# Layer 2: VectorE turns the probabilities in 32x32 blocks, DMAs exchange the groups of 32 partitions by way of DRAM, and GpSimd makes the low parts

## The chip, the cores and the metric

The kernel runs on one core of a Trainium2 chip. The metric is the device time of one execution in microseconds (us), as a median of several runs. The engines are called by their names in the profile: PE (TensorE, matmuls and transposes), DVE (VectorE), ACT (ScalarE), POOL (GpSimd) and SP (SyncE, which issues all the DMAs here). Each engine works through its own list in a fixed order; an instruction that has to wait holds up all that stand behind it on its engine.

## What is computed

A two-layer encoder over 1024 tokens of width 1024, in fp32. Both layers run projections, several attentions, a gate and an output projection. The change touches the attentions of layer 2:

```python
def odd_layer(x, mem_n, ...):
    h = rmsnorm(x, norm_g)
    q1, q2, k1, k2, v, xq, gate = _split(h @ w_in, ODD_SPLITS)
    lam = ...
    y_c = diff_attention_blocked(q1, q2, k1, k2, v, lam, table)   # 6 heads
    y_c = rmsnorm(y_c, subln_g) * (1.0 - lam_init)
    y_x = memory_cross_attention(xq, mem_n, w_mem_kv)             # 4 heads
    y = jnp.concatenate([y_c, y_x], axis=-1) * jax.nn.silu(gate)
    return x + y @ w_out

def diff_attention_blocked(q1, q2, k1, k2, v, lam, table):
    # for each head and each block of 128 queries
    s = einsum("ibqhd,ibshd->ibhqs", qi, kk) * D ** -0.5
    p = softmax(s + bias)
    w = p[0] - lam * p[1]
    return einsum("bhqs,bshe->bqhe", w, v)
```

## The kernel before

Every fp32 operand of a large product is split into a high part (rounded to PE's fp32r) and a low part (the rest), and a product is the sum of two or three products of such parts. The sequence is 8 blocks of 128 queries.

**Steps and pairs.** Layer 2 runs 8 steps of memory attention (four heads side by side, 256 memory tokens each) and then 6 heads × 8 steps of differential attention, one step per query block. Two steps of neighbouring blocks form a pair: 4 pairs, then 24. In all these steps a tile e of 128 queries x 1024 fp32 probabilities has to be transposed, so that the product with the values can sum over the keys: PE does this in 8 transposes of 128x128 (te, L580), each half of them into one PSUM tile; ACT rounds the half to the high part (L347), DVE subtracts it to give the low part (L348). The parts go into the tiles PT. There is one PT per pair.

**The loop.** `run_steps` (L475) writes the program. Its iteration i writes, for several steps at once: the hooks (loads of weights; `early.step`, which splits a piece of the output weights, wor on load, wos on ACT L270 and POOL L271); the hop of step i−1, a DMA that copies the finished e into a tile er of the type that PE's transposes want (`word_copy`); the scores of step i (sc, L1505 and L1514), bias and minimum on DVE (L1520), Exp on ACT (L1523); matmuls of the projections of later heads as filling (acc, L329, whose weights wr are split by DVE into wh, L241, and by POOL into wl, L243); the posts of an earlier pair; s3, the product of a pair with the values (oc, 16 matmuls, L1545 and L1547), lag + 1 iterations after the step; s2, the transposes, lag iterations after it; and the finish of step i on DVE (L1528 to L1532), which makes e = p0 − c·p1. The lag is 2.

**Behind oc.** ACT copies half of the sum out of PSUM (L1550), DVE adds the other half to give O (L1551). The post d1 sums squares on PE (ssqc, L1563) and POOL takes the power −1/2 (rz2, L231). The post d2 spreads that over the partitions on PE (rbcc, L1576), DVE multiplies O with it (L1578), and POOL multiplies into the gate tile (gy, L1581).

**Order and buffers.** The functions above give the order in which the program is written; a scheduler of the language then decides the order on each engine, within the dependences. `issue_after` sets one instruction behind another. The finish of a step is set so behind the last subtraction of s2 (`late=True`, `behind`). oc and acc share two PSUM buffers (tag A), the scores have two, PT one per half, er two, wr and wor share two.

Of the kernel before, what the change touches and what calls it, by code (L numbers as in the profile page):

```python
# [12 lines left out]
F32 = mybir.dt.float32  # L13
F32R = mybir.dt.float32r
AF = mybir.ActivationFunctionType
ALU = mybir.AluOpType
AX = mybir.AxisListType

P = 128
S = 1024  # L20
# [135 lines left out]
def encoder_kernel(ctx, tc, A):  # L156
# [39 lines left out]
    for t in (spare, edge):  # L196
# [12 lines left out]
    memT_d = [dr.tile([P, KT, MEM], F32R, name="memT%d" % i) for i in range(2)]  # L209
    wo_d = [[[dr.tile([P, 8, 512], F32R, name="wo%d%d%s" % (l, nh, c)) for c in "hl"] for nh in range(2)]  # L210
            for l in range(2)]
    vec_d = dr.tile([6, 512], F32, name="vec_d")
    skew_d = dr.tile([6, P, 512], F32, name="skew_d")

# [174 lines left out]

    def open_main(stack, side, l):  # L390
        M = Main()
        M.ne, M.xbufs = 0, 0
        M.wide = l == 1
        M.pl = pool(stack, "main%d" % l, side)
        M.cfg = (dict(Q=(1024, 4), K=4, KL=4, V=1, gy=4, sg=3, er=3) if l == 0
                 else dict(Q=(512, 8), K=4, KL=2, V=2, gy=2, sg=5, er=2))
        return M
# [77 lines left out]
    def run_steps(steps, jobs, hooks=None, pace=None):  # L475
        n = len(steps)
        posts = deque()
        p2 = p3 = 0
        finish = None
        for i in range(n + LAG + 1):  # L480
            behind = None
            if jobs is not None:
                jobs.step = i
            if hooks:
                hooks(i)
            if 0 < i <= n and steps[i - 1].hop:
                steps[i - 1].hop()
            if i < n:
                if steps[i].need:
                    jobs.ensure(*steps[i].need)  # L490
                finish = steps[i].s1()
            f = steps[min(i, n - 1)].fill
            if jobs is not None:
                if half[0] and len(wout) >= 8 and jobs.projected():
                    f = pace(i)
                two = f > 1 and p3 < n and p3 + steps[p3].lag + 1 <= i and steps[p3].s3b is not None
                jobs.pull(f - f // 2 - two)
                if hooks:
                    hooks(-1)
            for q in list(posts):  # L500
                q.pop(0)()
                if not q:
                    posts.remove(q)
            if p3 < n and p3 + steps[p3].lag + 1 <= i:
                st, p3 = steps[p3], p3 + 1
                if st.s3 is not None:
                    if st.need3:
                        jobs.ensure(*st.need3)
                    r = st.s3()
                    if r:  # L510
                        posts.append(r)
                    if st.s3b is not None:
                        jobs.pull(two)
                        st.s3b()
            if p2 < n and p2 + steps[p2].lag <= i:
                behind = steps[p2].s2()
                p2 += 1
            if finish:
                with (tc.issue_after(behind.ins) if behind is not None else nullcontext()):
                    finish()  # L520
                finish = None
            if jobs is not None:
                jobs.pull(f // 2)
                if hooks:
                    hooks(-1)
        while posts:
            for q in list(posts):
                q.pop(0)()
                if not q:
                    posts.remove(q)  # L530

    class Step:
# [2 lines left out]
        need3 = ()  # L535
        lag = 2
        hop = None
        s3 = None
        fill = 0

# [26 lines left out]
            e[0] = t  # L567
        return f

    def dense_s2(M, e, st, late=False):  # L570
        def f():
            if st.sub == 0:
                st.grp["pt"] = new_pt(M)
            h, lo = st.grp["pt"]
            for j in range(2):
                T = ps_t("te")
                to, idt = (T.bitcast(F32R), identr) if e[0].dtype == F32R else (T, ident)
                for i in range(4):
                    k = 4 * j + i
                    nc.tensor.transpose(to[:, i * P:(i + 1) * P], e[0][:, k * P:(k + 1) * P], idt)  # L580
                Tv = T.rearrange("p (k c) -> p k c", k=4)
                o = slice(st.sub * P, st.sub * P + P)
                r = split_to(h[:, 4 * j:4 * j + 4, o], lo[:, 4 * j:4 * j + 4, o], Tv)
            return r if late else None
        return f

    def mem_jobs(M, l, memT, X):
# [21 lines left out]
    def x_steps(M, X, gates, fill, qtile, ydst):  # L609
        steps = []  # L610
        for qb in range(8):
            st = Step()
            st.sub = qb % 2
            if st.sub == 0:
                grp = {}
            st.grp = grp
            e = [None]
            st.fill = fill

            def s1(qb=qb, e=e):  # L620
                kh, kl = X["kh"], X["kl"]
                Sp = ps_s("sx").rearrange("p (h m) -> p h m", h=4)
                for h in range(4):
                    qt, qc = qtile(h, qb)
                    qk(Sp[:, XPOS[h], :], qt, qc, kh[:, h, :], kl[:, h, :], 0, MEM)
                mn = stat("mn4", 4)
                nc.vector.tensor_reduce(out=mn, in_=Sp, op=ALU.min, axis=AX.X)
                et = new_e(M)
                ev = et.rearrange("p (h m) -> p h m", h=4)
                z = stat("z4", 4)  # L630
                for h in range(4):
                    nc.scalar.activation(ev[:, h, :], Sp[:, h, :], AF.Exp, bias=mn[:, h:h + 1],
                                         scale=-1.0, accum_out=z[:, h:h + 1])
                def finish():
                    rz = stat("rz4", 4)
                    nc.vector.reciprocal(rz, z)
                    for h in range(4):
                        nc.scalar.activation(ev[:, h, :], ev[:, h, :], AF.Copy, scale=rz[:, h:h + 1])
                    e[0] = et
                return finish  # L640
            st.s1 = s1
            st.hop = word_copy(M, e)
            st.s2 = dense_s2(M, e, st)
            if st.sub == 1:
                def s3(qb=qb, grp=grp):
                    v = X["v"]
                    ph, pl_ = grp["pt"]
                    S2 = ps_s("ox")
                    for p in range(2):
                        acc = S2[:, p * 512:p * 512 + 512]  # L650
                        for j in range(2):
                            h = 2 * p + j
                            n = 0
                            for kt in range(2):
                                for pt in (ph, pl_):
                                    nc.tensor.matmul(acc[:, j * 256:j * 256 + 256], v[:, kt, h, :],  # L656
                                                     pt[:, 2 * XPOS[h] + kt, :], start=(n == 0), stop=(n == 3))
                                    n += 1
                    for p in range(2):
                        acc = S2[:, p * 512:p * 512 + 512]  # L660
                        t = M.at.tile([P, 256], F32, tag="yt", name="yt", bufs=2)
                        for j in range(2):
                            a = slice(j * 64, j * 64 + 64)
                            nc.scalar.copy(t[a, :], acc[64 - j * 64:128 - j * 64, j * 256:j * 256 + 256])
                        for j in range(2):
                            a = slice(j * 64, j * 64 + 64)
                            nc.vector.tensor_tensor(out=t[a, :], in0=acc[a, j * 256:j * 256 + 256], in1=t[a, :],
                                                    op=ALU.add)
                        g = gates[6 + p][:, (qb - 1) * P:(qb + 1) * P]
# [812 lines left out]
    for h in range(6):  # L1482
        for qb in range(8):
# [8 lines left out]
            def s1(h=h, qb=qb, e=e, grp=grp):  # L1492
# [33 lines left out]
                def finish():  # L1526
# [4 lines left out]
                                                   op0=ALU.mult, op1=ALU.mult)  # L1531
                    nc.vector.scalar_tensor_tensor(out=es[0], in0=es[1], scalar=c, in1=es[0],  # L1532
                                                   op0=ALU.mult, op1=ALU.add)
                    e[0] = es[0]
                return finish
            st.s1 = s1
            st.hop = word_copy(M, e)
            st.s2 = dense_s2(M, e, st, True)
            if st.sub == 1:
                def s3(h=h, qb=qb, grp=grp):  # L1540
                    ph, pl_ = grp["pt"]
# [132 lines left out]
```

## Time and profile before

| | |
|---|---|
| three runs | 1223.57, 1226.14, 1230.64 us; median 1226.14 |
| the profiled execution's span | 1228.9 us |
| PE busy in it | 1196.5 us (97%) |
| DVE, ACT, POOL busy | 801.1 (65%), 663.1 (54%), 436.3 (36%) |
| layer 2's attention | about 680 to 1162 us of the span |
| the output projection of layer 2 behind it | from 1161.95 us on |

The profile is of one execution. A line "L329 PE MATMUL acc<-h,wh ..." names the line of the kernel that is printed above, the engine, the operation and the tiles; behind the bar stand the busy time and the mean duration in ns, and then how long the engine was idle just before such instructions and who released it. The chain of waits follows the end of the execution back, at each step to what released the instruction.

### The profile page before, as it was taken

How to read it: one execution, taken by the hardware profiler on the slowest of the kernel's cores; microseconds unless marked ns; L12 is line 12 of the kernel's file. 1: busy time of each engine (PE TensorE's matmuls, PEld its weight loads, DVE VectorE, ACT ScalarE, POOL GpSimd, SP SyncE). 2: the span in 40 equal slices, each digit the busy share in tenths (PEclk: the TensorE clock that was granted, in tenths of full speed). 3: DMA queues.
4: the chain of work that ended last, by engine and by line, in shares of the span. 5: the costliest groups of instructions: out<-in, count | busy, mean ns of one | idle time of the engine just before them, and what ended most of it. 6: DMA issues, size and time to landing. Idle time of an engine off the chain costs nothing.

```text
span 1228.9 us, 19560 instructions
## 1 busy us (share of the span) xinstructions
PE 1196.5 (97%) x6614; PEld 988.4 (80%) x6614; DVE 801.1 (65%) x1495; ACT 663.1 (54%) x1477; POOL 436.3 (36%) x414
## 2 busy tenths in 40 slices
PE   6999999999999999999999999999999999999997
PEld 5788888888888777888888777777787777777886
DVE  5547665377778878635365866766767767667544
ACT  6248754366667766636157744555545454445332
POOL 5023365366665455437112222333143231301100
PEclk9999999999999999999999999999999999999999
DMA  6664445545465565457645445355363452468354
GB/s 257 200 194 147 163 172 163 166 160 207 163 233 209 208 227 191 151 196 237 186 158 156 153 146 164 121 183 163 124 187 125 153 171 105 149 212 285 121 192 155
DMA packets 114304, 216.70 MB, mean 176 GB/s; under 512 B 13302, under 2 KB 47478, under 8 KB 114204
## 3 DMA queue, kind: packets, MB, share of 16 engines
q1 hardware_dynamic: 114060, 215.25, 52.5%
q8 instruction: 53, 0.87, 0.3%
q14 instruction: 47, 0.39, 0.1%
q10 hardware_dynamic: 144, 0.20, 0.0%
HBM read 87.71 MB, written 39.86 MB: 104 GB/s over the span
## 4 chain that ended last, share of the span: by engine, by line
PE 47%; DVE 2%; DMA 1%; issue 1%; ACT 1%; POOL 0%; POOLq 0%; SPq 0%; DVEq 0%; ACTq 0%
PE acc L329 24%; PE po L702 5%; PE oc L1545 3%; PE sc L1505 3%; PE te L580 3%; PE sc L1514 2%; PE pre L702 2%; PE oc L1547 2%; DMA wr<-in_w_in 1%; PE ssqc L1563 1%; PE ox L656 0%; PE rbcc L1576 0%; PE tv L439 0%; PE sx L543 0%; DVE e L1520 0%
## 5 line engine op out<-in xcount | busy, mean ns | idle before, releaser
L329 PE MATMUL acc<-h,wh 128*128 128x512 f32 x1536 | 499.5, 398 | 1.6 <-DVE h L351 0.8
L329 PEld LDWEIGHTS acc<-h,wh 128*128 128x128 f32 x1536 | 282.4, 188 | 65.7 <-issue 7.9
L329 PE MATMUL acc<-h,wl 128*128 128x512 f32 x768 | 303.8, 396 | 1.5 <-POOL wl L243 1.2
L243 POOL TENSOR_TENSOR wl<-wr,wh 128x512 fp32r<-128x512 f32 x94 | 124.8, 1329 | 286.3 <-DVE wh L241 155.0
L1523 ACT ACTIVATE e<-e,mn 128x1024 f32<-128x1024 f32 x96 | 110.0, 1148 | 117.0 <-DVE mn L1520 116.9
L329 PEld LDWEIGHTS acc<-h,wl 128*128 128x128 f32 x768 | 144.3, 188 | 34.9 <-issue 4.4
L1114 POOL TENSOR_TENSOR e<-e,rz 128x1024 f32<-128x1024 f32 x48 | 91.6, 1910 | 84.2 <-DVE rz L1113 57.8
L1520 DVE CUSTOM_DVE_ANT_0 e<-sc,toep 128x1024 f32<-128x1024 f32 x96 | 113.5, 1218 | 8.0 <-PE sc L1514 7.3
L580 PEld LDWEIGHTS te<-identr,er 128*128 128x128 f32 x896 | 92.2, 143 | 18.8 <-PE sa L543 2.2
L580 PE MATMUL te<-identr,er 128*128 128x128 f32 x896 | 99.9, 246 | 4.3 <-DVE O L1578 1.4
L348 DVE TENSOR_TENSOR PT<-te,PT 128x512 fp32r<-128x512 f32 x112 | 74.3, 687 | 42.8 <-ACT PT L347 39.2
L241 DVE CAST wh<-wr 128x512 fp32r<-128x512 f32 x112 | 58.2, 522 | 42.9 <-PE acc L329 17.3
L348 DVE TENSOR_TENSOR PTl<-te,PTh 128x512 fp32r<-128x512 f32 x112 | 74.0, 684 | 9.4 <-ACT PTh L347 8.9
L1545 PE MATMUL oc<-PT,v 128*128 128x512 f32 x192 | 69.8, 403 | 0.7 <-DVE ckl L1420 0.7
L1532 DVE SCALAR_TENSOR_TENSOR e<-e,mr 128x1024 f32<-128x1024 f32 x48 | 66.3, 1381 | 1.5
L347 ACT CAST PT<-te 128x512 fp32r<-128x512 f32 x112 | 62.7, 589 | 7.2 <-PE te L580 6.7
L347 ACT CAST PTh<-te 128x512 fp32r<-128x512 f32 x112 | 62.2, 586 | 7.9 <-PE te L580 7.1
L702 PE MATMUL po<-woh,yh 128*128 128x512 f32 (+1 forms) x172 | 65.7, 382 | 0.0
L702 PE MATMUL po<-woh,yl 128*128 128x512 f32 (+1 forms) x172 | 65.5, 381 | 0.0
L702 PE MATMUL po<-wol,yh 128*128 128x512 f32 (+1 forms) x172 | 65.3, 380 | 0.0
L1105 DVE TENSOR_REDUCE mn<-sb 128x1 f32<-128x1024 f32 x48 | 58.3, 1216 | 7.0 <-PE sb L543 6.6
L350 ACT ACTIVATE yh<-yr 128x256 fp32r<-128x256 f32 (+2 forms) x56 | 24.0, 447 | 66.2 <-DMA yr<-ysc 37.5
(211 smaller groups left out, 2358.7 us busy)
## 6 DMA issues: line engine op xcount, KB each, us to landing
er<-e SPq DMA_DIRECT2D x112, 512.0 KB, 3.0
wr<-in_w_in SPq DMA_DIRECT2D x96, 256.0 KB, 3.0
ysc<-gy SPq DMA_DIRECT2D x16, 512.0 KB, 2.7
cq<-sg SPq DMA_DIRECT2D x64, 128.0 KB, 2.5
ck<-sg SPq DMA_DIRECT2D x48, 128.0 KB, 2.3
er<-e SPq DMA_DIRECT2D x12, 384.5 KB, 2.6
xpsc<-xh SPq DMA_DIRECT2D x18, 256.0 KB, 2.6
xr<-xpsc SPq DMA_DIRECT2D x9, 512.0 KB, 3.6
```

Source lines behind the costliest of these rows:

```text
L243: (nc.vector if fast else nc.gpsimd).tensor_tensor(out=lo, in0=raw, in1=hi, op=ALU.subtract)
L329: lastmm[0] = nc.tensor.matmul(acc, a, b[:, k, c0:c0 + n], start=(i == 0), stop=(i == 23))
L347: nc.scalar.copy(hi, src)
L348: return nc.vector.tensor_tensor(out=lo, in0=src, in1=hi, op=ALU.subtract)
L580: nc.tensor.transpose(to[:, i * P:(i + 1) * P], e[0][:, k * P:(k + 1) * P], idt)
L702: lastmm[0] = nc.tensor.matmul(acc, a, b, start=(start and n == 0), stop=(stop and n == 2))
L1105: nc.vector.tensor_reduce(out=mn, in_=Sp, op=ALU.min, axis=AX.X)
L1114: nc.gpsimd.tensor_tensor(out=et, in0=et, in1=rz.to_broadcast([P, 1024]), op=ALU.mult)
L1520: nc.vector.tensor_tensor_reduce(out=et, in0=Sp, in1=toeps[h][:, w0:w0 + 1024], scale=1.0, scalar=BIG, op0=ALU.add, op1=ALU.min, accum_out ...
L1523: nc.scalar.activation(et, et, AF.Exp, bias=mn[:, m:m + 1], scale=-1.0, accum_out=z[:, m:m + 1])
L1532: nc.vector.scalar_tensor_tensor(out=es[0], in0=es[1], scalar=c, in1=es[0], op0=ALU.mult, op1=ALU.add)
L1545: nc.tensor.matmul(acc, V[:, kt, 0, :], ph.both[:, kt, :], start=(kt == 0), stop=(kt == 7), skip_group_check=True)
```

## The change

In layer 2 alone (`M.wide`), PE's transposes are replaced by three steps that together give the same tiles PT:

1. At the end of the finish DVE turns e within blocks of 32x32 in one instruction, into the second e tile of the step (`blocks_turned`, L575 of the changed kernel). The blocks are laid out so that the 1024 words of a partition are four runs of 256.
2. The hop writes that tile to DRAM (`turned_out`, 512 KB per step; three buffers that take a pair each). A new entry, fetch, two iterations after the step, reads it back for both steps of a pair, once per pair: four DMAs of 256 KB, each for 32 partitions in runs of 256 words, which exchanges the groups of 32 partitions (`turned_in`). There is one er tile for a pair.
3. s2 has no PE work: ACT rounds from er to the high part (L607), four times a pair, and POOL subtracts to give the low part (L608), four times a pair, instead of DVE (`turned_s2`).

The lag is 3 instead of 2, so s2 comes three iterations after the step and oc four. The `late` ordering is gone. Below line 570 the changed kernel's lines are higher by 52 as a rule (L1581 is L1633), above it by one.

```diff
@@ run_steps
             if 0 < i <= n and steps[i - 1].hop:
                 steps[i - 1].hop()
+            if 1 < i <= n + 1 and steps[i - 2].fetch:
+                steps[i - 2].fetch()
...
+    turn_d = [dr.tile([2, P, S], F32, name="turn_d%d" % i) for i in range(3)]
...
+    def blocks_turned(dst, src):
+        nc.vector.transpose(out=dst.rearrange("p (c k j) -> p k c j", c=4, k=8),
+                            in_=src.rearrange("p (k c j) -> p k c j", c=4, k=8))
+
+    def turned_out(M, e, st):
+        def f():
+            if st.sub == 0:
+                M.nturn = (M.nturn + 1) % len(turn_d)
+            st.grp["turn"] = turn_d[M.nturn]
+            dma(st.grp["turn"][st.sub], e[0])
+        return f
+
+    def turned_in(M, st):
+        def f():
+            if st.sub == 0:
+                return
+            t = M.at.tile([P, 2, 4, 256], F32, tag="er", name="er", bufs=1)
+            src = st.grp["turn"].rearrange("s (g i) (c x) -> c i (s g) x", g=4, c=4)
+            for c in range(4):
+                dma(t[32 * c:32 * c + 32].rearrange("p s g x -> p (s g) x"), src[c])
+            st.grp["er"] = t
+        return f
+
+    def turned_s2(st):
+        def f():
+            if st.sub == 0:
+                st.grp["pt"] = new_pt(M)
+            h, lo = st.grp["pt"]
+            er = st.grp["er"][:, st.sub].rearrange("p g (k j) -> p k g j", k=8)
+            for j in range(2):
+                ks = slice(4 * j, 4 * j + 4)
+                o = slice(st.sub * P, st.sub * P + P)
+                hv, lv = (t[:, ks, o].rearrange("p k (g j) -> p k g j", g=4) for t in (h, lo))
+                nc.scalar.copy(hv, er[:, ks])
+                nc.gpsimd.tensor_tensor(out=lv, in0=er[:, ks], in1=hv, op=ALU.subtract)
+        return f
+
+    def turn_pairs(M, e, st):
+        st.lag = 3
+        st.hop = turned_out(M, e, st)
+        st.fetch = turned_in(M, st)
+        st.s2 = turned_s2(st)
...
@@ the steps of memory attention, at the end of finish
                     e[0] = et
+                    if M.wide:
+                        e[0] = new_e(M)
+                        blocks_turned(e[0], et)
...
-            st.hop = word_copy(M, e)
-            st.s2 = dense_s2(M, e, st)
+            if M.wide:
+                turn_pairs(M, e, st)
+            else:
+                st.hop = word_copy(M, e)
+                st.s2 = dense_s2(M, e, st)
...
@@ the steps of differential attention
-                    e[0] = es[0]
+                    blocks_turned(es[1], es[0])
+                    e[0] = es[1]
...
-            st.hop = word_copy(M, e)
-            st.s2 = dense_s2(M, e, st, True)
+            turn_pairs(M, e, st)
```

The order on three engines at one place, the first pair of the fourth head, where the head before ends. On POOL before, from the power of one pair (rz2) to that of the next (gy is the product into the gate, wos and wl are low parts of weights, toep the bias of the next head):

```order
L231 TENSOR_TENSOR rz2_10905<-z2_10902,nhalf_78 128x2
L271 TENSOR_TENSOR wos_10945<-wor_10943,wos_10945 128x256
L243 TENSOR_TENSOR wl_10971<-wr_10968,wh_10970 128x512
L1581 TENSOR_TENSOR gy_10573<-O_10813,gy_10573 128x256
L243 TENSOR_TENSOR wl_10977<-wr_10974,wh_10976 128x512
L271 TENSOR_TENSOR wos_11069<-wor_11067,wos_11069 128x256
L1474 COPY toep_11295<-far_83 128x768 x2
L231 TENSOR_TENSOR rz2_11114<-z2_11111,nhalf_78 128x2
```

Here POOL has only gate products and weights, and behind gy stand pieces of weights. On POOL after:

```order
L232 TENSOR_TENSOR rz2_10732<-z2_10729,nhalf_78 128x2
L1526 COPY toep_10981<-far_83 128x768 x2
L1633 TENSOR_TENSOR gy_10332<-O_10637,gy_10332 128x256
L608 TENSOR_TENSOR PT_10644<-er_10575,PT_10644 128x4x128
L608 TENSOR_TENSOR PT_10645<-er_10575,PT_10645 128x4x128
L608 TENSOR_TENSOR PT_10644<-er_10575,PT_10644 128x4x128
L608 TENSOR_TENSOR PT_10645<-er_10575,PT_10645 128x4x128
L272 TENSOR_TENSOR wos_10675<-wor_10673,wos_10675 128x256
L244 TENSOR_TENSOR wl_10700<-wr_10697,wh_10699 128x512
L244 TENSOR_TENSOR wl_10706<-wr_10703,wh_10705 128x512
```

The four low parts of the next pair (two tiles PT, two steps) now stand on POOL, and they stand behind the gy product of the pair before them.

On PE before, at the same place, with the last filling, rbcc of the one pair and the start of oc of the next:

```order
L329 MATMUL acc<-h,wl 128x512
L329 MATMUL acc<-h,wh 128x512
L1576 MATMUL rbcc<-ident,rz_10905 128x128 x2
L1545 MATMUL oc<-PT,v 128x512
L1547 MATMUL oc<-PT,v 128x256
L1545 MATMUL oc<-PT,v 128x512
```

Here oc stands directly behind rbcc. On PE after:

```order
L330 MATMUL acc<-h,wh 128x512
L1628 MATMUL rbcc<-ident,rz_10732 128x128 x2
L330 MATMUL acc<-h,wh 128x512
L330 MATMUL acc<-h,wl 128x512
L330 MATMUL acc<-h,wh 128x512 x2
L330 MATMUL acc<-h,wl 128x512
L330 MATMUL acc<-h,wh 128x512 x2
L330 MATMUL acc<-h,wl 128x512
L1597 MATMUL oc<-PT,v 128x512
L1599 MATMUL oc<-PT,v 128x256
```

Eight matmuls of the projections (acc) now stand between rbcc and oc.

On DVE before, around the two instructions that deal with O:

```order
L241 CAST wh_10970<-wr_10968 128x512
L1578 SCALAR_TENSOR_TENSOR O_10813<-O_10813,misc_84,rbcc_10997 128x256
L241 CAST wh_10976<-wr_10974 128x512
L1551 TENSOR_TENSOR O_11019<-oc_11002,O_11019 128x256
L348 TENSOR_TENSOR PT_11026<-te_11028,PT_11026 128x4x128
L348 TENSOR_TENSOR PT_11027<-te_11035,PT_11027 128x4x128
L1528 RECIPROCAL rz_11042<-mn_10950 128x1
L1530 SCALAR_TENSOR_TENSOR mr_11044<-mn_10950,misc_84,rz_11042 128x1
```

Here one cast stands between O's multiplication and the addition of the next O, and the low parts of PT follow. On DVE after:

```order
L1584 SCALAR_TENSOR_TENSOR e_10786<-e_10789,mr_10846,e_10786 128x1024
L575 STREAM_TRANSPOSE e_10789<-e_10786 128x8x4x32
L1630 SCALAR_TENSOR_TENSOR O_10637<-O_10637,misc_84,rbcc_10809 128x256
L352 SCALAR_TENSOR_TENSOR sg_10753<-acc_10709,sg_10752 128x512
L242 CAST wh_10699<-wr_10697 128x512
L242 CAST wh_10705<-wr_10703 128x512
L1603 TENSOR_TENSOR O_10831<-oc_10814,O_10831 128x256
L352 SCALAR_TENSOR_TENSOR sg_10859<-acc_10792,sg_10858 128x512
```

The low parts of PT are gone from DVE; the turn (STREAM_TRANSPOSE) stands ahead of O's multiplication, and two casts of weights and one of the projection's results stand between that and the addition of the next O.

More of the change, by code (lines that the diff above doesn't have):

```diff
@@ L391, in open_main @@
         M = Main()
-        M.ne, M.xbufs = 0, 0
+        M.ne, M.xbufs, M.nturn = 0, 0, 0
         M.wide = l == 1
@@ L537, in encoder_kernel @@
         hop = None
+        fetch = None
         s3 = None
@@ L568, in word_copy, with dense_s2 @@
         return f
-    def dense_s2(M, e, st, late=False):
+    def blocks_turned(dst, src):
[36 more added lines that the diff above has]
+        st.s2 = turned_s2(st)
+    def dense_s2(M, e, st):
         def f():
@@ L582, in f @@
                 o = slice(st.sub * P, st.sub * P + P)
-                r = split_to(h[:, 4 * j:4 * j + 4, o], lo[:, 4 * j:4 * j + 4, o], Tv)
-            return r if late else None
+                split_to(h[:, 4 * j:4 * j + 4, o], lo[:, 4 * j:4 * j + 4, o], Tv)
         return f
```

## Prediction

> **What bounds the kernel now.** I read the busy table of the stages first, then the chain of waits inside one stage, then the groups by line there, then what POOL waits for.
>
> ```profile
> core 0: us, PE busy (x) PEld busy (x) DVE busy (x) ACT busy (x) POOL busy (x), PEclk, DMA share, GB/s
> 680.00:1162.00 482.00, 478.79 (x2537) 378.27 (x2537) 338.31 (x615) 243.30 (x496) 125.49 (x131) 1.00 0.49 161
> ```
>
> The stretch from 680 to 1162 us is the attention of layer 2, where nearly all of the change lies. PE is busy for 478.79 of 482 us at full clock, so it sets the pace: what PE no longer does is gained whole, and each microsecond that PE waits is lost whole. DVE has 30% of the stretch free, POOL 74%.
>
> ```profile
> 906.22 0.38 PE te L580 x4
> 906.60 0.53 PE acc L329 x2
> 907.13 0.29 PE te L580 x4
> ...
> 910.70 0.91 PE sc L1505 x4
> 911.60 0.66 PE sc L1514 x4
> 912.26 3.86 PE acc L329 x16
> 916.12 0.22 PE rbcc L1576 x2
> 916.34 0.23 PE oc L1545
> 916.57 0.12 PE oc L1547
> ...
> 919.13 0.65 PE te L580 x8
> 919.78 1.92 PE acc L329 x8
> ```
>
> This is the chain of waits for the steps around 910 us (start, length, what). It never leaves PE. One pair of query blocks holds 16 transposes te, 0.38 + 0.29 + 0.65 = **1.32 us**, and the products oc, 16 matmuls of (0.23 + 0.12) a couple, 2.80 us in all, stand straight behind rbcc. An oc reads PT, whose low part DVE made long before, so nothing holds it.
>
> **What goes.** Layer 2 has 4 pairs of memory attention and 24 of differential attention: 28 × 1.32 = **37.0 us** of PE go. Since the chain runs through every te, I count all of it.
>
> **DVE and ACT.** Per step two PT subtractions (L348) leave DVE and one turn of 128x1024 comes.
>
> ```profile
> L348 DVE TENSOR_TENSOR PT<-te,PT 128x512 fp32r<-128x512 f32 x100 | 66.5, 688 | 40.3 <-ACT PT L347 36.8
> L347 ACT CAST PT<-te 128x512 fp32r<-128x512 f32 x100 | 56.3, 589 | 6.6 <-PE te L580 6.2
> L1532 DVE SCALAR_TENSOR_TENSOR e<-e,mr 128x1024 f32<-128x1024 f32 x48 | 66.3, 1381 | 1.5
> L241 DVE CAST wh<-wr 128x512 fp32r<-128x512 f32 x40 | 17.8, 446 | 12.9 <-DMA wr<-in_w_in 9.8 <-PE acc L329 1.9 <-issue 0.9
> ```
>
> The third column group is busy time and mean ns. No turn stands in the trace. It lies between two casts of 512 (2 × 0.446 = 0.89) and the L1532 pass over 1024 (1.38). I take 1.22, as nearer to the full pass because both move 1024 words a lane in one instruction. DVE then gives 1.38 and takes 1.22: even, and DVE has room at both ends. The Trainium skill ("VectorE: DVE Perf Modes", § The three transpose paths) speaks against a change of this kind: VectorE's transpose makes separate 32x32 blocks only, TensorE's a whole 128x128, and a plain DMA that does a transpose by strides is 19 times slower than the DMA's own transpose when the inner destination stride is large. Here the DMAs exchange runs of 256 words, not single words, so its condition is not met; by that rule a fetch would never be hidden, and no row here shows such a DMA. ACT's casts stay (589 ns from PSUM, from SBUF hardly more); ACT is 50% busy.
>
> **POOL.** Four subtractions of 128x512 a pair move to POOL. The same operation at the same size stands there as wl.
>
> ```profile
> L243 POOL TENSOR_TENSOR wl<-wr,wh x94: 1259/1290/2377, 12.8 to 1068.5; 128x512 fp32r<-128x512 f32 x94
> L271 POOL TENSOR_TENSOR wos<-wor,wos 128x256 fp32r<-128x256 f32 x32 | 27.4, 858 | 49.5 <-ACT wos L270 49.1
> L1114 POOL TENSOR_TENSOR e<-e,rz 128x1024 f32<-128x1024 f32 x48 | 91.6, 1910 | 84.2 <-DVE rz L1113 57.8
> L1474 POOL COPY toep<-far 128x768 f32<-128x768 f32 x8 | 6.4, 827 | 14.6 <-DVE mn L1520 14.6
> POOL gy L1581 <- DVE O L1578: 78.5, 19, 7.5
> ```
>
> The first row has min/median/max ns. I take the median, **1.29 us**, each; the new one differs in strides alone. The lower end is half of L1114 (0.96), the upper 2.38. Per pair that is 5.2 us more on POOL, which has some 15 of 20 free. Its busy time is no bound; its order is. The last row says that gy waited for DVE's O 19 times in this execution, up to 7.5 us. Before, nothing urgent stood behind gy. In the changed order the four subtractions of pair p+1 stand behind the gy of pair p in 13 of 24 pairs, and in those PE comes to oc of pair p+1 after little else than rbcc of pair p. How long gy takes from rbcc is in the timeline:
>
> ```profile
> 1014.95 0.38 PE L1576 MATMUL rbcc<-ident,rz 128*128 128x128 f32 x2
> 1015.60 0.48 DVE L1578 SCALAR_TENSOR_TENSOR O<-O,misc,rbcc 128x256 f32<-128x256 f32 x1
> 1016.16 0.75 POOL L1581 TENSOR_TENSOR gy<-O,gy 128x256 f32<-128x256 f32 x1 [5.46 <-DVE O L1578]
> ```
>
> From the start of rbcc to the end of gy: 1016.91 − 1014.95 = 1.96 us. The first oc needs the first half of both blocks, three subtractions: 3 × 1.29 = 3.87. So oc may start **5.83 us** after rbcc. PE has rbcc itself (0.22) and what stands between. The list, pair by pair of the order:
> - three pairs with 8 acc between (1.92): 5.83 − 0.22 − 1.92 = 3.69 each, 11.1;
> - the first pair with a toep copy (0.83) and two wl (2.58) among the subtractions: 4.5 before the first oc, and (2.58 + 1.29 − 1.40) = 2.5 before the second half of them, 7.0;
> - one with a subtraction already ahead of gy: 2.4; one with 8 acc and two score matmuls between (2.4): 3.2; two with 8 acc and ten score matmuls (3.9) but one wos (0.86) ahead of the fourth subtraction: 2.4 each, 4.8;
> - the last three pairs of the program, with four, four and two po matmuls (0.23 each) between: 4.7, 4.7, 5.1, together 14.5;
> - two with 8 us or more between: nothing.
>
> Sum **43 us**, against nothing before (the chain above shows rbcc and oc adjoining). If PE itself is late, its rbcc is late as well and the distance stays.
>
> **The accumulators.** oc and the projections' acc share two PSUM buffers, and an oc buffer is free when DVE has added O (L1551). Before, 14 of 24 O adds stand straight behind O's multiplication on DVE, most others with one cast between. Now 13 of 24 have the 128x1024 pass (L1532) within two rows ahead, and others two casts whose loads wait on SP for POOL's reads. At the low end the pass is done before oc's 2.80 us are over: nothing. At the upper end one pass of 1.28 to 1.38 in each of the 24 pairs: 31 to 33 us. I take half, **16 us**, since oc's 2.80 us hide the multiplication and about one of the two long instructions.
>
> **The DMAs.**
>
> ```profile
> er<-e SPq DMA_DIRECT2D x48, 512.0 KB, 2.9
> woh<-wo10h SPq DMA_DIRECT2D x8, 256.0 KB, 4.9
> wol<-wo10l SPq DMA_DIRECT2D x8, 256.0 KB, 5.6
> wr<-in_w_in SPq DMA_DIRECT2D x40, 256.0 KB, 3.2
> ...
> L175 SPq DMA_DIRECT2D er<-e x136: 464/472/614, 77.2 to 1146.0; - x136
> ...
> SPq L175 <- DVE e L1532: 78.6, 32, 9.8
> ```
>
> The hop stays one issue per step, to DRAM instead of SBUF (2.9 us; the 16 engines are half busy). New are four issues of 256 KB a pair, behind the hop on SP. The reads from DRAM land in 3.2 to 5.6 us, and SP takes 0.47 an issue. I take 3.2 + 4 × 0.47 = 5.1, with 7.5 as the other end. The last row shows how SP already stands still for DVE's e, 32 times; the loads wr and wor behind it then wait too. The third step of lag covers 10 us (482 us over 48 steps), so I put nothing on the pairs, and **5 us** on the two ends, where the first and the last pair meet the longer way (turn 1.22, fetch 5.1, three subtractions 3.87, less the 3.4 below that are idle already and some 2 of po): between 0 and 10.
>
> ```profile
> 1157.38 3.39 issue
> 1160.77 0.70 POOL rz L231
> ```
>
> **Sum.** −37.0 + 43 + 16 + 5 = +27 on the profiled span of 1228.9 is 1256. That execution lay 2.8 above the median of the runs (1226.14) and inside their spread; taken off, **1253 us**, 2.2% slower.
>
> **Rivals.**
> *GpSimd is quick enough: faster.* Place: the stretch from gy to the first oc in the 13 pairs. Price: each 0.1 us of a subtraction is worth some 3.5 us, as some 35 subtractions in all stand between a gy and an oc that waits. With 16 for the accumulators gone and 5 for the ends, it decides from about 0.98 us per subtraction; at 0.75, what gy takes for half the size, the sum is −37 + 24 + 5 = −8, 1218 us. For it: L1114 does 512 words in 0.96. Against it: 94 wl of the same operation never took less than 1.259.
> *The waits at oc and no more: a draw.* The adds are in time and the ends cost nothing to 5: −37 + 43 + 3 = +9 at most, or less if a few of the 13 waits are shorter: 1226 to 1235, taken at 1231. For it: DVE has 30% free.
> *The round trip or POOL is slow: much slower.* There is one er tile for a pair, so the next fetch waits for the last subtraction. With fetches of 10 us instead of 5.1 some 3 us per pair come on top wherever POOL has no time in hand: 12 to 24 pairs, 36 to 72, 1289 and more. The same comes of subtractions of 1.7 us when they collide with DVE's passes: 35 × 0.4 = 14 directly, and as much again through the accumulators. Two rows show such a collision:
>
> ```profile
> 1048.96 1.28 DVE L1532 SCALAR_TENSOR_TENSOR e<-e,mr 128x1024 f32<-128x1024 f32 x1
> 1049.03 2.38 POOL L243 TENSOR_TENSOR wl<-wr,wh 128x512 fp32r<-128x512 f32 x1 [1.95 <-DMA wr<-in_w_in]
> ```
>
> POOL's wl began 0.07 us behind DVE's pass and took 2.38 instead of 1.29, as if it had stood still until the pass was over. The Trainium skill ("SBUF — State Buffer", § SBUF: two separate sides) says just that: a VectorE instruction with two SBUF inputs and a GpSimd one that reads SBUF exclude each other for a whole instruction. These two rows agree with it; by that rule each of the 48 passes that meets a subtraction costs one of the two up to 1.3 us.
> *The change does not do what it says*: not so, the rows of the order have no te in layer 2.
>
> **How the numbers follow.** Forecast 0.62, gain 0.15, draw 0.08, much slower 0.15. The forecast's own range comes from the accumulators' 0 to 33 and the ends' 0 to 10: 1232 to 1275. The range reaches to 1215 and 1288 and leaves out about half of the gain and most of the much slower case. A change within 0.5% (6 us) can't be told from none with this kernel's runs; the draw lies across that bound. Faster 0.15, same 0.10, slower 0.75.
>
> **What would show it.** Right: te gone from layer 2 with 37 us of PE; PE idle ahead of oc with POOL's subtraction as releaser, some 40 us over about 13 pairs, and nothing like it in the others; the new POOL row at 1.29; PE idle ahead of acc with DVE's O add as releaser, about 16. Wrong: POOL rows below 1 us; PE waiting for oc in none of the 13; or fetches that land in 10 us and POOL's subtractions waiting for er.

## The result, and the profile after

| | before | after |
|---|---|---|
| median of the runs | 1227.06 us (4 runs, 1223.57 to 1230.64) | 1391.53 us (4 runs, 1385.1 to 1393.86) |
| ratio | | 1.134, 95% interval 1.130 to 1.137 |
| profiled span | 1228.9 us | 1392.1 us |
| granted TensorE clock, mean over the span | 0.996 | 0.931 |

The change makes the kernel 164 us slower, six times what was forecast (27) and outside the range (1215 to 1288). First the busy table by stretches, of the changed kernel (busy us of each engine with the count of instructions, then granted clock, DMA share, GB/s):

```profile
core 0: us, PE busy (x) PEld busy (x) DVE busy (x) ACT busy (x) POOL busy (x), PEclk, DMA share, GB/s
0.00:640.00 640.00, 617.22 (x3564) 524.16 (x3565) 416.00 (x789) 374.13 (x857) 297.74 (x266) 1.00 0.56 191
640.00:850.00 210.00, 153.42 (x661) 118.29 (x660) 110.04 (x166) 86.06 (x196) 82.19 (x72) 0.82 0.50 143
850.00:1150.00 300.00, 258.86 (x1139) 195.87 (x1138) 188.68 (x302) 129.51 (x262) 151.18 (x132) 0.93 0.58 171
1150.00:1392.00 242.00, 190.87 (x807) 147.39 (x806) 110.45 (x183) 75.12 (x163) 62.53 (x57) 0.85 0.55 174
```

Layer 1, up to 640 us, is as it was. From there on no engine is full: PE at 73, 86 and 79% (before: 99% in the attention), DVE at 46 to 63%. What bounds the kernel is no longer an engine, but engines that wait for each other. And the clock, which was 1.00 in this stage, stands at 0.82 to 0.93 in these stretches.

The whole can be accounted for on PE. For each matmul from 640 us on I took the time to the start of the next one: the median of its kind in the kernel before is work, a small excess is slow clock, a larger one is waiting (where the border between the two is set moves some 3 us from one to the other). Work went from 587 to 547 us (−40: te is gone), waiting from 4 to 169 (+165), slow clock from 2 to 41 (+39). Together +164.

Then the groups by line (busy, mean ns, idle before), and what engines waited for (us in total, times, longest), of the changed kernel:

```profile
L608 POOL TENSOR_TENSOR PT<-er,PT 128x512 fp32r<-128x512 f32 x112 | 151.8, 1382 | 95.4 <-ACT PT L607 94.7 <-DMA xh<-x1sc 0.7
L575 DVE STREAM_TRANSPOSE e<-e 128x1024 f32<-128x1024 f32 x53 | 65.8, 1241 | 9.7 <-ACT e L684 8.8
L1597 PE MATMUL oc<-PT,v 128*128 128x512 f32 x192 | 86.4, 477 | 37.8 <-POOL PT L608 37.1 <-DVE gy L461 0.7
```

```profile
...
POOL PT L608 <- ACT PT L607: 94.7, 16, 16.9
...
DVE wh L242 <- DMA wr<-in_w_in: 62.9, 17, 14.5
...
ACT wos L271 <- DMA wor<-in_w_out: 38.5, 17, 7.5
PE oc L1597 <- POOL PT L608: 37.1, 11, 6.0
...
PE sc L1557 <- DVE mn L1572: 27.2, 14, 5.0
```

The durations are as forecast: a turn 1.24 us, a subtraction 1.38. PE's wait at oc for POOL's subtractions is there too, 37.1 us in 11 waits, and 43 was forecast. That looks like a hit and isn't one, as the experiments show. The new rows are the others. DVE's casts of weights wait 62.9 us for the load (9.8 in the attention before), ACT's for wor, POOL for ACT. One such place, in the timeline (start, length; the idle time before it and its releaser in brackets):

```profile
799.48 0.26 ACT L1619 ACTIVATE z<-ssqc,es 128x1 f32<-128x1 f32 x1 [8.13 <-PE ssqc L1615]
799.63 1.13 ACT L607 CAST PT<-er 128x512 fp32r<-128x512 f32 x2
800.32 2.49 POOL L608 TENSOR_TENSOR PT<-er,PT 128x512 fp32r<-128x512 f32 x2 [16.89 <-ACT PT L607]
...
805.87 2.48 POOL L244 TENSOR_TENSOR wl<-wr,wh 128x512 fp32r<-128x512 f32 x2
...
808.38 0.33 SPq L175 DMA_DIRECT2D wr<-in_w_in  x1
...
811.28 0.43 DVE L242 CAST wh<-wr 128x512 fp32r<-128x512 f32 x1 [14.46 <-DMA wr<-in_w_in]
811.62 1.28 DVE L352 SCALAR_TENSOR_TENSOR sg<-acc,sg 128x512 fp32r<-128x512 f32 x2
...
812.36 1.22 PE L330 MATMUL acc<-h,wh 128*128 128x512 f32 x2 [12.92 <-DVE sg L352]
```

Read from the end: PE stands still for 12.92 us because DVE hasn't emptied an accumulator (sg). DVE could have, but a cast of weights stands ahead of it in DVE's list and waits 14.46 us for its load. The load goes out at 808.38, when POOL's wl has freed its buffer. POOL is late because a subtraction ahead of wl waited 16.89 us for ACT's cast of PT, and that stood in ACT's list behind z, which waited 8.13 us for PE's ssqc. No instruction here is long. Each list holds something back behind a thing that isn't needed yet.

### The profile page after: what moved, and what is told of

Read it like the earlier page. It is cut to its first block, busy times and chain, and to the rows that moved or that the text cites. A ratio compares the mean times of both kernels' runs of the same rounds, so it can differ in the third digit from the quotient of the medians.

```text
span 1392.1 us, 18783 instructions
## 1 busy us (share of the span) xinstructions
PE 1220.4 (88%) x6166; PEld 985.7 (71%) x6166; DVE 825.2 (59%) x1439; ACT 664.8 (48%) x1477; POOL 593.6 (43%) x526
## 4 chain that ended last, share of the span: by engine, by line
PE 24%; issue 10%; POOL 8%; DMA 8%; DVE 5%; SPq 2%; ACT 2%; POOLq 0%; DVEq 0%; ACTq 0%
PE acc L330 12%; POOL PT L608 6%; PE po L754 4%; DMA er<-turn_d 3%; SPq L175 2%; PE oc L1597 2%; DMA wor<-in_w_out 1%; DMA wr<-in_w_in 1%; DVE e L1584 1%; PE sc L1566 1%; PE pre L754 1%; PE sc L1557 1%; PE oc L1599 1%; POOL wl L244 1%; DVE e L1572 1%
## 5 line engine op out<-in xcount | busy, mean ns | idle before, releaser
L330 PE MATMUL acc<-h,wh 128*128 128x512 f32 x1536 | 510.1, 407 | 35.9 <-DVE sg L352 12.9
L330 PEld LDWEIGHTS acc<-h,wh 128*128 128x128 f32 x1536 | 293.0, 194 | 106.6 <-DVE sg L352 13.0
L608 POOL TENSOR_TENSOR PT<-er,PT 128x512 fp32r<-128x512 f32 x112 | 151.8, 1382 | 95.4 <-ACT PT L607 94.7
L242 DVE CAST wh<-wr 128x512 fp32r<-128x512 f32 x112 | 69.1, 623 | 92.0 <-DMA wr<-in_w_in 70.5
L1597 PE MATMUL oc<-PT,v 128*128 128x512 f32 x192 | 86.4, 477 | 37.8 <-POOL PT L608 37.1
L1557 PE MATMUL sc<-ck,cq 128*128 128x512 f32 x192 | 64.8, 440 | 37.1 <-DVE mn L1572 27.2
L232 POOL TENSOR_TENSOR rz<-z,nhalf 128x2 f32<-128x2 f32 x24 | 22.2, 926 | 147.0 <-ACT z L1619 147.0
L1597 PEld LDWEIGHTS oc<-PT,v 128*128 128x128 f32 x192 | 44.3, 231 | 53.7 <-POOL PT L608 41.7
L575 DVE STREAM_TRANSPOSE e<-e 128x1024 f32<-128x1024 f32 x56 | 69.5, 1240 | 9.7 <-ACT e L684 8.8
L1557 PEld LDWEIGHTS sc<-ck,cq 128*128 128x128 f32 x192 | 36.3, 204 | 53.4 <-DVE mn L1572 35.0
L1584 DVE SCALAR_TENSOR_TENSOR e<-e,mr 128x1024 f32<-128x1024 f32 x48 | 71.5, 1489 | 1.4
```

The lines of the kernel that those rows point to most:

```text
L330: lastmm[0] = nc.tensor.matmul(acc, a, b[:, k, c0:c0 + n], start=(i == 0), stop=(i == 23))
L575: nc.vector.transpose(out=dst.rearrange("p (c k j) -> p k c j", c=4, k=8), in_=src.rearrange("p (k c j) -> p k c j", c=4, k=8))
L608: nc.gpsimd.tensor_tensor(out=lv, in0=er[:, ks], in1=hv, op=ALU.subtract)
L1557: full = nc.tensor.matmul(Sps[m][:, c], C[h][(m, qb // 4)][:, qc], C[h]["k"][m][:, c], start=True, stop=False)
L1597: nc.tensor.matmul(acc, V[:, kt, 0, :], ph.both[:, kt, :], start=(kt == 0), stop=(kt == 7), skip_group_check=True)
```

## The experiments

Three theories at first: P, the prediction's (POOL's subtractions stand behind gy); R, a ring through the one er tile of a pair; X, the way through DRAM.

Runs 1 to 11, 13 and 16 are one execution each; the repeated ones spread by 4 to 8 us, so a few us between single runs say nothing. An edit also lets the scheduler write a new order, so that runs 1 to 11 and 16 can change more than their edit shows. Only in runs 12 to 15 is the order of every engine given.

**1. Low parts on DVE again** (`nc.gpsimd.tensor_tensor(out=lv, ...)` becomes `nc.vector...`, and nothing else).

> One part undone: the low parts of layer 2's PT are made by DVE again, all else as changed (1391.5). Theory P (POOL's order: the subtractions stand behind gy and hold oc, and the rest follows from those waits): the 42 us of PE idle ahead of oc go, and with them some of the slow clock, 1330 to 1350. Theory R (the one er tile of a pair: POOL's last subtraction, then the four fetches on SP, then ACT, then POOL again form a ring, and SP's queue with weights stands behind it): the ring gets shorter by 4 x 0.7 us and by POOL's queue, so it falls too, to 1340 to 1370, but the long idle stretches in the memory-attention steps (PE busy about 14 to 19 of 25 us between 685 and 810 us) stay. Theory X (the way through DRAM is too long by itself): 1380 to 1395.

Measured 1349.7, inside the ranges of both P and R, so the time doesn't choose between them. The waits do: POOL has no subtractions left, and PE still waits ahead of oc, by the same account as above 40 us against 42 in the changed kernel. P expected these to go; only the releasers are others now.

**2. gy on DVE** (`nc.gpsimd.tensor_tensor(out=g, in0=O, in1=g, op=ALU.mult)` becomes `nc.vector...`).

> The product into the gate tile (gy) of the differential steps goes from POOL to DVE, so that no subtraction on POOL can stand behind it; the subtractions stay on POOL. P: PE idle ahead of oc falls from 42 to under 10 us, 1340 to 1355. R: the middle of the attention gets a little faster, start and end do not, 1370 to 1390. X: 1380 to 1395.

Measured 1376.3; P expected 1340 to 1355, and R's range (1370 to 1390) holds it. Nothing stands behind gy on POOL any more, and the wait ahead of oc falls from 42 to 30 us, not to under 10. The order of PE, ACT and SP is all but that of the changed kernel here, so this is close to a test of gy alone: P is a small part.

**3. An er tile per step.**

```diff
-            if st.sub == 0:
-                return
-            t = M.at.tile([P, 2, 4, 256], F32, tag="er", name="er", bufs=1)
-            src = st.grp["turn"].rearrange("s (g i) (c x) -> c i (s g) x", g=4, c=4)
+            t = M.at.tile([P, 4, 256], F32, tag="er", name="er", bufs=2)
+            src = st.grp["turn"][st.sub].rearrange("(g i) (c x) -> c i g x", g=4, c=4)
             for c in range(4):
-                dma(t[32 * c:32 * c + 32].rearrange("p s g x -> p (s g) x"), src[c])
+                dma(t[32 * c:32 * c + 32], src[c])
...
```

> Each step has its own er tile (half the size, two buffers, the same room), fetched by four DMAs of 128 KB per step instead of four of 256 KB per pair; low parts on POOL as changed. P: nothing at oc changes, 1380 to 1400 (four issues more per pair cost SP 1.9 us). R: the first step's subtractions no longer hold the second step's fetch, the stretches in the memory-attention steps and at the end shrink, 1310 to 1350. X: 1385 to 1400.

Measured 1390.9, where P and X put it and R didn't (1310 to 1350): R falls as the main cause.

**4. No DRAM.** The hop of the third run copies the turned tile into er in one DMA, and there is no fetch, so the exchange of the groups is left out.

> Like the run with an er tile per step, but the exchange by way of DRAM is left out: the hop copies the turned tile straight into er by one DMA of 512 KB, as before the change, so groups of 32 partitions are not exchanged. P: as the run with an er tile per step, within 15 us. R: somewhat below it, since the ring loses the fetch. X: 1230 to 1280, most of the loss gone with the second transfer.

Measured 1222.5, below X's range (1230 to 1280) and far from the others. All of the loss goes with the exchange. X comes nearest; but what of the exchange? Four runs on that, with L for the length of the way and N for the number and kind of DMAs.

**5. Fetch from a fixed place** (`src = x_d[0:P]...`), so that it waits for no hop.

> As the run with an er tile per step (1390.9), but the fetch reads 128 rows of the input x in DRAM instead of the turned tile, in the same four DMAs of 128 KB; the hop still writes the turned tile to DRAM. So the number of issues and the bytes are the same, and the fetch waits for no hop; the data are not those of the step. Theory L (what costs is the length of the way: the fetch can be issued only when the hop has landed, and SP's queue stands meanwhile): 1225 to 1260. Theory N (what costs is the number of issues, the bytes and their short runs): 1360 to 1395.

Measured 1387.0, in N's range.

**6. One fetch DMA** (`dma(t, st.grp["turn"][st.sub]...)` instead of the loop over c).

> As the run with an er tile per step, but the fetch is one DMA of 512 KB in runs of 4 KB that takes the tile back as it was written; the groups of 32 partitions are not exchanged. L: the wait for the landing is still there, 1350 to 1390. N: three of four issues and the short runs are gone, 1240 to 1300.

Measured **1216.1**, below the kernel before, with the whole way through DRAM and the wait for the hop's landing in it, and with a DMA share in the attention (0.67) above that of every run before it (0.58 at most). It is below N's range too (1240 to 1300); the exchange of the groups is left out.

**7. Four DMAs without DRAM** (the copy of run 4 in four pieces of 32 partitions).

> As the run without DRAM (1222.5), but the copy from the turned tile to er is made by four DMAs of 128 KB in place of one of 512 KB. L: 1222 to 1235. N: at three issues more per step of 0.47 us on SP, the half of what the exchange adds in issues, 1280 to 1330.

Measured 1357.7, above N's range (1280 to 1330): the second transfer isn't needed for the loss, the four pieces bring it without one.

**8. One more step of lag.**

> As the run with an er tile per step, with the right exchange, but the fetch is written one iteration later and the lag is 4 instead of 3, so a step has 10 us more between hop and use. L: the hop has landed when SP comes to the fetch, 1240 to 1300. N: 1380 to 1400.

Measured 1391.6. L is out: in 5 the wait is taken away, in 8 it has 10 us more, and neither helps; in 6 it is there and costs nothing. But N didn't sit well with the trace. The four pieces of run 7 land in 2.4 us each, and SP issues 218 of 500 us there (640 to 1140). How early the weights are ready says more. A job of filling uses two low parts wl; I set the end of its first one against the job's first matmul, for the last 20 jobs. The median is 21.4 us before the matmul in the kernel before, 21.7 and 19.4 in runs 4 and 6; 4.2 in the changed kernel, −0.5 in run 3 and −1.0 in run 7. In run 3 PE waits for them. The lists themselves say the same without a clock: before, and in runs 4 and 6, a weight's load stands on SP 3.9 to 4.9 steps ahead of its use on PE, in the changed kernel and runs 3 and 7 2.9 to 3.0. The scheduler had made another order. Hence theory S: it is the order; against it H: the four DMAs cost on the chip.

**9. Priority for the weights** (`with tc.high_priority():` around `load_w` in layer 2).

> The changed kernel with one difference: the loads of projection weights in layer 2 and their two splits (wr, wh, wl) get priority in the scheduler, so that they are placed as early as buffers allow; nothing is computed otherwise and no DMA is added or removed. In the runs so far the low part wl is ready some 21 us before its first matmul in the kernel before and in the two fast runs (1222.5 and 1216.1), and 4 us before to 2 us after it in the slow ones. Theory S (the scheduler, counting four more DMAs a pair, places the loads so late that the order has no reserve left): the lead comes back, 1230 to 1290. Theory H (the four DMAs cost on the chip by themselves, by SP's time or by limits on what is under way): 1375 to 1395.

Measured 1379.8, in H's range (1375 to 1395) and far above S's (1230 to 1290). The lead came back only to 9.2 us; the waits ahead of acc fell from 42 to 18 us by the account on PE, but oc's wait for POOL's subtractions rose from 37.1 to 52.4. S as it was put there, by the weights alone, is not borne out; that one reserve was bought with another is a guess.

**10. SP's list as written** (`with tc.manual_schedule(engines={SP})` around the loop).

> The changed kernel with SP's list in layer 2 in the order in which the program is written, instead of the scheduler's; the other engines' lists are the scheduler's. S: weights stand on SP about as late as in the changed kernel, so some gain at best where a fetch stands ahead of a weight, 1300 to 1390; if the lead of wl comes back to over 15 us the time is under 1290. H: 1375 to 1395.

Measured 1407.3, above both ranges, with a lead of 4.0 us. It decides nothing between S and H.

**11. Three tiny DMAs in the kernel before.**

```diff
             dma(t.bitcast(F32), e[0])
+            if M.wide:
+                for i in range(3):
+                    dma(tiny_d[i], e[0][:32, 8 * i:8 * i + 8])
...
```

> The kernel before, with three DMAs of 1 KB added behind every hop of layer 2, from the hop's tile to DRAM, that nothing uses: as many issues as the fetch by four adds per step, hardly any bytes. S: the lead of wl falls under 10 us, 1290 to 1370. H by bytes or by landing times: 1225 to 1235. H by SP's issue time (3 x 0.4 us of some 10 us per step, SP issuing a third of the time now): 1225 to 1250, with the lead unchanged.

Measured 1226.6, lead 21.4 us. S had expected the lead to fall and 1290 to 1370, and missed. The number of issues alone costs nothing, and it doesn't upset the scheduler either.

**12 and 13. The orders exchanged.** Only this tells S from H. Run 12 is run 3 with the order of run 6 on all engines, run 13 is run 6 with the order of run 3. ORDER holds, for each engine, the places of its instructions as the scheduler put them in the other variant; an instruction is queued behind the one ahead of it in that list:

```diff
...
+    for text in ORDER.values():
+        raw = zlib.decompress(base64.b64decode(text))
+        at, last = 0, None
+        for d in struct.unpack("<%di" % (len(raw) // 4), raw):
+            at += d
+            i = kept[at]
+            while i is not None:
+                if last is not None:
+                    tc.add_manual_dep(i, last.name, mybir.DependencyInfo(
+                        mybir.DependencyClass.NoSync, mybir.DependencyReason.DATA), reason="order")
+                last, i = i, behind_of.get(i.name)
```

> The kernel with an er tile per step and the right exchange by four DMAs (1390.9), but every engine's list in the order that the scheduler made for the variant with one fetch DMA per step (1216.1); the four DMAs stand where the one stood. The two lists are the same on PE, DVE, ACT and POOL. Theory S (the order is what costs): 1215 to 1245. Theory H (the four DMAs of 32 partitions cost on the chip): 1340 to 1395.

> The reverse: the variant with one fetch DMA per step (1216.1, groups not exchanged), every engine's list in the order that the scheduler made for the variant with four (1390.9). S: 1360 to 1395. H: 1210 to 1235.

Measured **1229.2** (ratio to before 1.002, 95% interval 1.000 to 1.004) and **1392.5**. With the same instructions, the order is worth 162 us; in the same order, one DMA or four are worth 13 at most (1216.1 and 1229.2) or nothing (1392.5 and 1390.9). H is out. PE's waits for weights go with the order too: here are two rows of run 3 and then the same two of run 13 (its lines are higher by 104), which has another fetch but run 3's order. Run 12 has no row of PE waiting for wl or wh.

```profile
PE acc L330 <- POOL wl L244: 22.4, 9, 4.4
...
PE acc L330 <- DVE wh L242: 15.1, 6, 3.7
```

```profile
PE acc L434 <- POOL wl L348: 23.5, 9, 4.4
...
PE acc L434 <- DVE wh L346: 15.1, 6, 3.7
```

The exchange moved the lists of all engines at once. Which engine's list, or which part of one, makes the difference is not shown.

**14. The fast order, low parts on DVE.**

> As the run in the fast order, with the right exchange, but the low parts are made by DVE instead of POOL, in the order that the scheduler makes for that variant with one fetch DMA. S, and POOL's subtractions cost something on top: 1195 to 1215. S, and POOL's subtractions cost nothing in a good order: 1213 to 1240. H: over 1300.

Measured **1209.1**, ratio 0.987 (0.984 to 0.989): 1.3% faster than the kernel before, with the right exchange. It is 20 us below run 12 (1229.2 − 1209.1). That is what moving the subtractions from POOL to DVE gives together with the order that the scheduler makes for it; how much of it is POOL's instructions alone is not shown.

**15. The changed kernel itself in a fast order**, that which the scheduler makes for it when a pair's fetch is one DMA.

> The changed kernel itself (one er tile per pair, four fetch DMAs of 256 KB per pair, low parts on POOL), with every engine's list in the order that the scheduler makes when the fetch is a single DMA; nothing else differs from the changed kernel (1391.5). S: 1220 to 1260, a little above the run with an er tile per step (1229.2), since the next fetch still waits for POOL's last subtraction. H, or the single er tile as a cost of its own: over 1300.

Measured **1238.8**, ratio 1.011 (1.009 to 1.014). Its rows, of the same views as above (its lines are higher by 101 to 103, so L711 is L608):

```profile
640.00:850.00 210.00, 191.15 (x897) 147.40 (x896) 141.73 (x226) 113.48 (x254) 116.89 (x103) 0.97 0.70 204
850.00:1150.00 300.00, 285.88 (x1365) 219.82 (x1363) 225.40 (x361) 152.67 (x310) 161.27 (x140) 1.00 0.75 225
```

```profile
...
POOL PT L711 <- ACT PT L710: 57.2, 15, 8.3
DVE wh L343 <- DMA wr<-in_w_in: 41.5, 21, 3.7
...
PE oc L1700 <- POOL PT L711: 0.8, 1, 0.8
```

```profile
L711 POOL TENSOR_TENSOR PT<-er,PT 128x512 fp32r<-128x512 f32 x112 | 147.7, 1344 | 61.7 <-ACT PT L710 57.2 <-DMA turn_d<-e 4.5
L1700 PE MATMUL oc<-PT,v 128*128 128x512 f32 x192 | 73.3, 418 | 6.9 <-DVE ckl L1575 2.7 <-DVE gy L562 1.8 <-DVE xh L903 1.4
```

PE is busy at 91 and 95%, the longest wait of a cast for weights is 3.7 us instead of 14.5, the clock is at 0.97 and 1.00, and oc hardly waits for a subtraction: 37.1 us in 11 waits in the changed kernel, 0.8 in one now, with the same subtractions on the same engine. They even stand straight behind a gy more often, three or four of them 16 times against 13. The account on PE is: work −39 against the kernel before, waiting +42, slow clock +6.

**16. Two queues** (`nc.scalar if c > 1 else None` as the engine that issues; er per step, low parts on DVE, the order left to the scheduler).

> A variant without a list written in: an er tile per step, low parts on DVE, and two of the four fetch DMAs of a step issued by ACT instead of SP, the order left to the scheduler. In its order the scores stand evenly ahead of oc (4 steps for 22 of 24 pairs, as in the fast variants; the slow ones vary from 3 to 6), but weights are loaded only 3.2 steps ahead of use (3.9 to 4.9 in the fast ones, 2.9 to 3.0 in the slow). S, if the even spacing decides: 1205 to 1250. S, if the lead of the weights decides: 1330 to 1400. H: over 1330.

Measured 1255.4, lead of wl 11.5 us. It lies just above the range for even spacing (1205 to 1250) and far below the other. That even spacing does most and the weights' lead the rest would fit, but one run doesn't show it. Run 14 has the same operations, but for the engine that issues two of the four DMAs, and takes 46 us less in its order.

## Why the prediction was right and wrong

- *te goes, 37.0 us*: right. PE's work is 40 us less in the changed kernel, 39 in run 15.
- *DVE's turn, 1.22 us, even on DVE*: right; 1.24 us, and DVE is nowhere the bound.
- *POOL's subtraction, 1.29 us* (0.96 to 2.38): right in kind, 1.38 in the changed kernel and 1.34 in run 15. DVE's pass beside it (L1584) went from a mean of 1381 to 1489 ns in the changed kernel, but only to 1388 in run 15, and it takes 1341 in run 14, which has no subtraction on POOL. So the collisions that the two rows of wl and L1532 showed cost at most some 0.15 us an instruction on average. The rule of the Trainium skill ("SBUF — State Buffer", § SBUF: two separate sides) that the prediction set beside those rows agrees in direction with the means.
- *The fetch, 5.1 us* (to 7.5): right, 5.6 from issue to landing; pieces of 128 KB in runs of 1 KB land in 3.1 us in run 12. The "19 times slower" of the Trainium skill ("VectorE: DVE Perf Modes", § The three transpose paths) doesn't show here; the prediction had said that its condition is not met.
- *43 us of waits at oc, because the subtractions stand behind gy*: the sum agreed (37.1 by the profile), by luck, since the cause did not. Taken off POOL in run 2, gy gave back 12 of the 42 that the account has ahead of oc; in run 15 the subtractions stand behind gy as before, and oc waits 0.8 us for them in all. The chain of 5.83 us was added up rightly, but it takes POOL's subtractions to be ready to run when gy is done. In the changed kernel they themselves waited 94.7 us for ACT's cast, up to 16.9 at a time.
- *16 us of waits for accumulators*: PE waits 42 us ahead of acc by the account, but only 5.8 of them by the profile for DVE's O add, which the prediction named. The two longest waits, 12.9 and 12.6 us, are for sg and ckl, standing behind casts that wait for loads (wh on DVE as shown above, wos on ACT).
- *"The third step of lag covers 10 us, so I put nothing on the pairs, and 5 us on the two ends"*: **this is the step that failed.** I took it that everything outside the 13 pairs keeps the reserve it had: weights 21 us early, every buffer free in time. By the start of oc, the third pair of differential attention was 70 us late already, the 15 pairs behind it lost another 49, and the last six another 45. Against a cost of 5, that is where most of the 164 is. The order that was compared at a few places was another order everywhere. Runs 12 and 13 show that the order makes the time, and run 15 that 153 of the 164 us are its price for this kernel (1391.5 − 1238.8). Which of the lost reserves weighs most stays open: run 9 brought part of the weights' lead back and gained 12 us.
- *No term for the clock*: an omission. Where PE waits, the granted clock is lower (0.82 where PE is busy 73%, 1.00 at 95%), +39 us. The stage that the prediction was read from couldn't show it, as PE hardly waited there.
- *Rivals*: "GpSimd is quick enough" needed subtractions below 0.98 us and found 1.38. "The round trip is slow" had the size nearest to the truth, 1289 and more, but not the mechanism: fetches land in 5.6 us, not 10, and run 15 holds the same round trip and the same single er tile at 1238.8.

In the order of run 15 the change thus costs 13 us against the kernel before: 39 saved, and some 52 given back. Estimates from runs 12 and 14, each in an order of its own, put 10 of these on er per pair (1238.8 − 1229.2) and 20 on POOL's subtractions. Without either, run 14 takes 1209.1. Why the scheduler gives up its reserve when large pieces of 32 partitions have to be placed, and not with tiny ones, stays open; the lists show that it does.

## What to carry to other kernels

When a scheduler decides the order, a change to a few instructions can change every engine's list. So compare the reserves of the lists before and after (how many steps ahead of use a load stands, how evenly the consumers stand behind their producers), not only the places that the diff touches. If a variant is slow without a full engine or a long instruction, give it the order of a fast variant and the other way round: two such runs tell the order from the operations, though not which list matters.

## What was not expected of the hardware

The granted clock follows PE's waits: 1.00 in the stage before, 0.82 in the stretch in which PE is 73% busy, 0.93 at 86%, and back to 1.00 at 95% in run 15; 39 us of slow clock stand beside the 165 us of waits. The record of the clock in these traces has two levels, full and half. From 640 us on the changed kernel has 23 pieces at half, 188 us together. In the 6.8 us ahead of each of them PE was busy for at most 78% of the time, in the median 59%, while the median of all such spans there is 98%. Run 15 has 5 such pieces, 24 us together.

And a high DMA share was no limit here: run 6 had 0.67 in the attention and was faster than the kernel before, and run 15 had 0.70 and 0.75 while PE waited 0.7 us for a DMA from 640 us on.
